# Low parts of the weights: a scalar-engine multiplication and an adding DMA in place of a vector subtraction

## The chip, the cores and the metric

The kernel runs on one core of a Trainium2 chip. A core has TensorE (PE, matrix products), VectorE (DVE), ScalarE (ACT), GpSimd (POOL) and SyncE (SP), each with its own queue of instructions that it takes strictly in order, and 16 DMA engines that are shared by all queues that issue transfers. The metric is the device time of one execution in microseconds (us).

## What is computed

Two layers of a sequence model over 512 tokens of width 1024, all in float32. Each layer has a token mixer (indexer-selected attention beside chunked gated linear attention), a residual with layer norm, a convolutional feed-forward network, and a second residual with layer norm. Cut to what matters here:

```python
def reference(x, positions, w_in, ...):
    for l in range(DEPTH):
        y = hybrid_mixer(x, positions, w_in[l], ..., p_attn[l], p_gla[l], w_mix_out[l], b_mix_out[l])
        x = layer_norm(DN_ALPHA * x + y, ln1_g[l], ln1_b[l])
        y = conv_ffn(x, w_up[l], conv_w[l], conv_b[l], w_down[l])
        x = layer_norm(DN_ALPHA * x + y, ln2_g[l], ln2_b[l])
    return x
```

Nearly all of the arithmetic is products of activations with weight matrices: w_in (1024 x 7256), p_attn, p_gla, w_mix_out, w_up (1024 x 5632) and w_down (2816 x 1024), for each layer.

## The kernel before

Every weight is streamed once, in 286 tiles of 128x1024 float32 (512 KB; two of them are 128x832). TensorE works on a rounded format (float32r), so a float32 operand is split in two: a high part, which is the value rounded, and a low part, which is the value minus the high part. A product is then three matmuls (mm3, lines 148 to 152): high by low, low by high, high by high.

A tile w has both parts side by side: w[:, 0] is the high one and w[:, 1] the low one. A tile's life is: SP issues the load of raw (line 130); ACT casts raw to the high part (line 144, in split); DVE subtracts the high part from raw into the low part (line 145); PE uses w in 24 matmuls of 512 columns (or 48 of 256). There are three buffers for raw (pool wraw) and five for w (pool wsp). So a load waits until raw has been read for the last time, three tiles before, and a cast waits until PE has done with the w of five tiles before.

pump (lines 125 to 135) issues load, cast and subtraction; weight calls it so that up to four tiles are ready ahead of their use, in the order that plan_all has laid down. The split of a tile is emitted at high priority: the framework's scheduler, which sets the order of each engine's queue when the kernel is built, puts it ahead of other work that is ready at the same time. The first tile of all is split in run (in two halves), not in pump. No caller of pump gives its argument parts.

Which of the two parts PE wants first depends on the stage. Where the weight is the moving operand (tm_chunk and closing: mixer projections, output products) the first matmul needs the low part. Where it is the stationary operand (fm_tile) the first needs the high part and the second the low one.

Most stages use a tile in one run and release it. Three places keep four tiles at once: the second half of closing (each of four token blocks goes over the same four tiles), the start of ffn (four tiles of w_up, first over tokens 0 to 255, then over 256 to 511) and the first product of layer 2 (iq, in two halves of the tokens). A closing is followed by one of the other two, so there the five slots come free late.

Beside the weights, POOL has little to do: constants at the start, the power in rstd (line 298; each layer norm of a token block has one, its argument comes from DVE and its result goes back to DVE), and 16 copies of 128 KB in twice (line 484), by DMA from POOL's queue.

Of the kernel before, what the change touches and what calls it, by code (L numbers as in the profile page):

```python
# [10 lines left out]
F32 = mybir.dt.float32  # L11
F32R = mybir.dt.float32r
I32 = mybir.dt.int32
AF = mybir.ActivationFunctionType
ALU = mybir.AluOpType
# [40 lines left out]
class Trunk:  # L56
# [68 lines left out]
    def pump(self, ahead, parts=None):  # L125
        while self.nsp < len(self.seq) and len(self.ready) < ahead:
            key, src, n = self.seq[self.nsp]
            self.nsp += 1
            raw = self.wraw.tile([128, n], F32, name=self.name("raw"), tag="raw")
            self.nc.sync.dma_start(raw.rearrange(src[1], **src[2]) if src[1] else raw, src[0])  # L130
            w = self.wsp.tile([128, 2, n], F32R, name=self.name("w"), tag="w")
            with self.tc.high_priority():
                for c in parts or (slice(0, n),):
                    self.split(w[:, 0, c], w[:, 1, c], raw[:, c])
            self.ready.append((key, w))

    def weight(self, key, keep=0):
# [872 lines left out]
```

## Time and profile before

| what | us |
|---|---|
| median of 3 runs (1798.42 to 1799.81) | 1798.6 |
| the profiled execution, its own time | 1798.15 |
| its span, first to last instruction | 1796.4 |
| PE busy | 1770.9 |
| DVE busy | 1150.0 |
| ACT busy | 758.4 |
| POOL busy | 35.6 |

The span is what the rows of the trace divide; the profiled execution took 1.75 us more than its span. TensorE's granted clock was 0.999 of full speed over the span. "Busy" of PE counts a matmul until its modelled end, so short waits between matmuls are not seen as idle time. In rows of groups and of time lines the operation is written with the program's names, output first: `w<-raw` writes w from raw. A line is that of kernel.py; split's lines 144 (ACT) and 145 (DVE) serve all splits, so weights are told apart by the names w and raw.

### The profile page before, as it was taken

How to read it: one execution, taken by the hardware profiler on the slowest of the kernel's cores; microseconds unless marked ns; L12 is line 12 of the kernel's file. 1: busy time of each engine (PE TensorE's matmuls, PEld its weight loads, DVE VectorE, ACT ScalarE, POOL GpSimd, SP SyncE). 2: the span in 40 equal slices, each digit the busy share in tenths (PEclk: the TensorE clock that was granted, in tenths of full speed). 3: DMA queues.
4: the chain of work that ended last, by engine and by line, in shares of the span. 5: the costliest groups of instructions: out<-in, count | busy, mean ns of one | idle time of the engine just before them, and what ended most of it. 6: DMA issues, size and time to landing. Idle time of an engine off the chain costs nothing.

```text
span 1796.4 us, 21646 instructions
## 1 busy us (share of the span) xinstructions
PE 1770.9 (99%) x8280; PEld 1436.5 (80%) x8280; DVE 1150.0 (64%) x2172; ACT 758.4 (42%) x1154; POOL 35.6 (2%) x57
## 2 busy tenths in 40 slices
PE   9999999999999999999999999999999999999997
PEld 7787787888888888888878877787888888888886
DVE  7899768733476553355768997786335765532556
ACT  6644657522225442144255456574232254422440
POOL 0000000000000000000000001000000000000000
PEclk9999999999999999999999999999999999999999
DMA  6222231233523322232332223212325233223331
GB/s 204 68 81 63 78 97 48 82 95 94 170 76 106 94 94 94 94 95 95 127 120 71 73 69 91 74 59 72 106 93 175 66 111 94 94 94 94 95 115 49
DMA packets 56980, 169.38 MB, mean 94 GB/s; under 512 B 6214, under 2 KB 6470, under 8 KB 56876
## 3 DMA queue, kind: packets, MB, share of 16 engines
q1 hardware_dynamic: 51312, 153.96, 27.5%
q10 hardware_dynamic: 4284, 11.94, 2.0%
q0 software_dynamic: 1280, 2.10, 0.6%
q8 instruction: 65, 1.06, 0.2%
q14 instruction: 39, 0.32, 0.1%
HBM read 161.68 MB, written 4.19 MB: 92 GB/s over the span
## 4 chain that ended last, share of the span: by engine, by line
PE 60%; DVE 5%; issue 3%; ACT 1%; POOL 1%; POOLq 0%; DVEq 0%; ACTq 0%
PE ps L152 19%; PE ps L150 19%; PE ps L151 19%; DVE w L145 1%; DVE u L741 1%; POOL rs L298 1%; PE ps L491 1%; PE ps L492 1%; PE ps L640 0%; DVE u L740 0%; DVE sc L525 0%; DVE bs L734 0%; DVE xT L145 0%; DVE u L853 0%; DVE u L145 0%
## 5 line engine op out<-in xcount | busy, mean ns | idle before, releaser
L145 DVE TENSOR_TENSOR w<-raw,w 128x1024 fp32r<-128x1024 f32 (+2 forms) x287 | 349.6, 1218 | 488.9 <-ACT w L144 488.2
L144 ACT CAST w<-raw 128x1024 fp32r<-128x1024 f32 (+2 forms) x287 | 299.8, 1045 | 482.9 <-PE ps L152 415.8
L150 PE MATMUL ps<-xT,w 128*128 128x512 f32 (+2 forms) x1232 | 475.4, 386 | 0.0
L152 PE MATMUL ps<-xT,w 128*128 128x512 f32 (+2 forms) x1232 | 472.6, 384 | 0.0
L151 PE MATMUL ps<-xT,w 128*128 128x512 f32 (+2 forms) x1232 | 472.2, 383 | 0.0
L152 PEld LDWEIGHTS ps<-xT,w 128*128 128x128 f32 (+1 forms) x1232 | 231.7, 188 | 48.1
L150 PEld LDWEIGHTS ps<-xT,w 128*128 128x128 f32 (+1 forms) x1232 | 231.9, 188 | 45.9
L151 PEld LDWEIGHTS ps<-xT,w 128*128 128x128 f32 (+1 forms) x1232 | 231.9, 188 | 45.4
L150 PE MATMUL ps<-w,u 128*128 128x512 f32 x480 | 190.3, 397 | 0.0
L152 PE MATMUL ps<-w,u 128*128 128x512 f32 x480 | 189.4, 395 | 0.0
L151 PE MATMUL ps<-w,u 128*128 128x512 f32 x480 | 189.3, 394 | 0.0
L150 PE MATMUL ps<-w,xT 128*128 128x512 f32 x448 | 179.7, 402 | 0.0
L152 PE MATMUL ps<-w,xT 128*128 128x512 f32 x448 | 177.9, 397 | 0.0
L151 PE MATMUL ps<-w,xT 128*128 128x512 f32 x448 | 176.6, 394 | 0.0
L144 ACT CAST u<-h 128x512 fp32r<-128x512 f32 x104 | 64.2, 620 | 199.6 <-DVE h L893 111.4
L150 PEld LDWEIGHTS ps<-w,u 128*128 128x128 f32 x480 | 90.4, 188 | 21.1 <-issue 0.3
L152 PEld LDWEIGHTS ps<-w,u 128*128 128x128 f32 x480 | 90.4, 188 | 21.0
L151 PEld LDWEIGHTS ps<-w,u 128*128 128x128 f32 x480 | 90.5, 188 | 20.5
L152 PEld LDWEIGHTS ps<-w,xT 128*128 128x128 f32 x448 | 84.3, 188 | 19.3
L150 PEld LDWEIGHTS ps<-w,xT 128*128 128x128 f32 x448 | 85.0, 190 | 18.0 <-DVE w L145 0.3
L151 PEld LDWEIGHTS ps<-w,xT 128*128 128x128 f32 x448 | 84.5, 189 | 16.2
L145 DVE TENSOR_TENSOR u<-h,u 128x512 fp32r<-128x512 f32 x104 | 71.3, 689 | 38.7 <-ACT u L144 38.4
(200 smaller groups left out, 2076.6 us busy)
## 6 DMA issues: line engine op xcount, KB each, us to landing
raw<-in_w_fm SPq DMA_DIRECT2D x160, 512.0 KB, 3.6
raw<-in_w_tm SPq DMA_DIRECT2D x55, 512.0 KB, 3.6
raw<-in_w_down SPq DMA_DIRECT2D x44, 512.0 KB, 3.4
raw<-in_w_mix_out SPq DMA_DIRECT2D x16, 512.0 KB, 3.4
raw<-in_p_attn SPq DMA_DIRECT2D x8, 512.0 KB, 3.8
u<-in_xT SPq DMA_DIRECT2D x8, 256.0 KB, 5.4
u<-u POOLq DMA_DIRECT2D x16, 128.0 KB, 2.8
u<-in_x ACTq DMA_DIRECT2D x4, 512.0 KB, 6.6
```

The source lines that it names most:

```text
L144: first = self.nc.scalar.copy(hi, src)
L145: self.nc.vector.tensor_sub(lo, src, hi.bitcast(F32))
L150: mm(out, lh, rl, start=start, stop=False)
L151: mm(out, ll, rh, start=False, stop=False)
L152: mm(out, lh, rh, start=False, stop=stop)
L298: self.nc.gpsimd.tensor_tensor(r, ve, self.nhalf[:, :n], ALU.pow)
L491: mm(out, q, k, start=True, stop=False)
L492: mm(out, q, kl, start=False, stop=True)
L741: nc.vector.scalar_tensor_tensor(x[:, c], x[:, c], r, b[:, c], op0=ALU.mult, op1=ALU.add)
```

## The change

In pump, the split of a tile is replaced. ACT casts raw to the high part as before; ACT then writes minus the high part into the low part's place; then a DMA issued from POOL's queue adds raw to what stands there, in place. raw minus high is again what the low part holds. split itself and all other uses of it stay as they are, and so does the first tile.

```diff
             with self.tc.high_priority():
-                for c in parts or (slice(0, n),):
-                    self.split(w[:, 0, c], w[:, 1, c], raw[:, c])
+                if parts:
+                    for c in parts:
+                        self.split(w[:, 0, c], w[:, 1, c], raw[:, c])
+                else:
+                    self.nc.scalar.copy(w[:, 0], raw)
+                    self.nc.scalar.mul(w[:, 1], w[:, 0].bitcast(F32), -1.0)
+                    self.nc.gpsimd.dma_start(w[:, 1], raw.bitcast(F32R), accum_op=ALU.add)
             self.ready.append((key, w))
```

In the changed kernel the cast is line 137, the multiplication 138 and the adding DMA 139; every later line of the old kernel has a number higher by 5. The scheduler lays the queues anew. POOL's queue grows by 285 DMAs, ACT's by 285 activations, DVE's loses 285 subtractions. Names of buffers are numbered in the order in which they are made, so the numbers of the two kernels differ.

ACT's queue at the start of the kernel, where the second, third and fourth weight tiles (raw_121, raw_132, raw_143) and the quarters of x transposed (u) arrive. Before:

```order
L144 CAST w_123<-raw_121 128x1024 [waits DMAHW5_49]
L144 CAST xT<-u_101 128x512 [waits DMAHW6_49]
L144 CAST xT<-u_102 128x512 [waits DMAHW7_49]
L144 CAST w_134<-raw_132 128x1024 [waits DMAHW0_49]
L144 CAST xT<-u_102 128x512 [waits DMAHW1_49]
L144 CAST xT<-u_103 128x512 [waits DMAHW2_49]
L144 CAST w_145<-raw_143 128x1024 [waits DMAHW3_49]
```

The same place in the changed kernel:

```order
L137 CAST w_123<-raw_121 128x1024 [waits DMAHW5_49]
L149 CAST xT<-u_101 128x512 [waits DMAHW6_49]
L138 ACTIVATE w_123<-w_123 128x1024 [waits Activation_49]
L149 CAST xT<-u_102 128x512 [waits DMAHW7_49]
L137 CAST w_135<-raw_133 128x1024 [waits DMAHW0_49]
L149 CAST xT<-u_102 128x512 [waits DMAHW1_49]
L138 ACTIVATE w_135<-w_135 128x1024 [waits Activation_49]
L149 CAST xT<-u_103 128x512 [waits DMAHW2_49]
```

A multiplication stands behind each cast of a weight, with one cast of xT between. PE's queue is the same in both kernels over this stretch.

POOL's queue at the conv-FFN's start in layer 1 (w_4479 is the first tile of w_up, w_4491, w_4503 and w_4701 the next three; rs are the norms of the four token blocks). Before there are only the norms' powers:

```order
L298 TENSOR_TENSOR rs_4441<-rs_4440,nhalf 128x1
L298 TENSOR_TENSOR rs_4492<-rs_4491,nhalf 128x1
L298 TENSOR_TENSOR rs_4550<-rs_4549,nhalf 128x1
L298 TENSOR_TENSOR rs_4608<-rs_4607,nhalf 128x1
L275 MEMSET h_7132 96x512
```

In the changed kernel:

```order
L139 DMA w_4479<-raw_4477 128x1024 [waits DMASW7_49,DMAHW3_49,PE_49,Activation_49]
L303 TENSOR_TENSOR rs_4520<-rs_4519,nhalf 128x1 [waits DVE_49]
L303 TENSOR_TENSOR rs_4571<-rs_4570,nhalf 128x1 [waits DVE_49]
L303 TENSOR_TENSOR rs_4629<-rs_4628,nhalf 128x1 [waits DVE_49]
L139 DMA w_4491<-raw_4489 128x1024 [waits DMASW0_49,DMAHW5_49,PE_49,Activation_49]
L139 DMA w_4503<-raw_4501 128x1024 [waits DMASW1_49,DMAHW6_49,PE_49,Activation_49]
L139 DMA w_4701<-raw_4699 128x1024 [waits DMASW2_49,DMAHW7_49,PE_49,Activation_49]
L303 TENSOR_TENSOR rs_4687<-rs_4686,nhalf 128x1 [waits DVE_49]
```

The last block's power has three adding DMAs ahead of it, which wait for ACT; these stand behind the powers of the first three blocks, which wait for DVE.

DVE's queue at the same place, the norm of the third token block (u_4253 before, u_4324 after). Before:

```order
L297 TENSOR_SCALAR rs_4549<-mv_4547 128x1 [waits DVE_49]
L740 SCALAR_TENSOR_TENSOR u_4253<-u_4253,mv_4547,u_4257 128x512
L145 TENSOR_TENSOR w_4414<-raw_4412,w_4414 128x1024 [waits DMAHW4_49,Activation_49]
L299 TENSOR_TENSOR rs_4551<-rs_4550 128x1 [waits Pool_49]
L740 SCALAR_TENSOR_TENSOR u_4253<-u_4253,mv_4547,u_4257 128x512
L145 TENSOR_TENSOR w_4425<-raw_4423,w_4425 128x1024 [waits DMAHW6_49,Activation_49]
L300 TENSOR_TENSOR rs_4551<-rs_4551,rs_4549 128x1 [waits DVE_49]
L145 TENSOR_TENSOR xT<-ps_4569,xT 128x4x128
L145 TENSOR_TENSOR w_4622<-raw_4620,w_4622 128x1024 [waits DMAHW7_49,Activation_49]
L301 TENSOR_SCALAR rs_4551<-rs_4551 128x1 [waits DVE_49]
```

In the changed kernel:

```order
L302 TENSOR_SCALAR rs_4628<-mv_4626 128x1 [waits DVE_49]
L745 SCALAR_TENSOR_TENSOR u_4324<-u_4324,mv_4626,u_4328 128x512
L304 TENSOR_TENSOR rs_4630<-rs_4629 128x1 [waits Pool_49]
L745 SCALAR_TENSOR_TENSOR u_4324<-u_4324,mv_4626,u_4328 128x512
L305 TENSOR_TENSOR rs_4630<-rs_4630,rs_4628 128x1 [waits DVE_49]
L150 TENSOR_TENSOR xT<-ps_4648,xT 128x4x128 [waits Activation_49]
L306 TENSOR_SCALAR rs_4630<-rs_4630 128x1 [waits DVE_49]
```

Three subtractions of weights that stood between the steps of this norm are gone.

## Rows read from the trace of the kernel before

**Rows 1.** The page: busy time, share of the span and instructions by engine.

```profile
PE 1770.9 (99%) x8280; PEld 1436.5 (80%) x8280; DVE 1150.0 (64%) x2172; ACT 758.4 (42%) x1154; POOL 35.6 (2%) x57
```

**Rows 2.** Windows: us, PE, PEld, DVE, ACT, POOL busy (x instructions), PEclk, DMA share, GB/s.

```profile
0.00:20.00 20.00, 18.47 (x70) 14.64 (x71) 13.87 (x32) 12.27 (x17) 3.44 (x18) 1.00 0.84 290
100.00:240.00 140.00, 135.73 (x697) 109.16 (x696) 119.52 (x295) 72.28 (x115) 7.60 (x10) 1.00 0.28 83
500.00:548.00 48.00, 46.97 (x312) 42.52 (x311) 36.43 (x70) 15.77 (x21) 3.91 (x4) 1.00 0.26 77
548.00:840.00 292.00, 292.00 (x1260) 236.73 (x1259) 151.62 (x179) 106.68 (x133) 1.51 (x3) 1.00 0.30 96
...
1740.00:1796.40 56.40, 46.73 (x202) 37.49 (x200) 32.84 (x65) 6.12 (x7) 3.93 (x4) 0.95 0.21 75
```

**Rows 3.** Groups by line and form: busy us, mean ns | idle before, releasers.

```profile
L145 DVE TENSOR_TENSOR w<-raw,w 128x1024 fp32r<-128x1024 f32 x283 | 346.2, 1223 | 486.4 <-ACT w L144 485.7
...
L144 ACT CAST w<-raw 128x1024 fp32r<-128x1024 f32 x283 | 296.8, 1049 | 480.5 <-PE ps L152 415.8 <-issue 41.1 <-DMA u<-in_ln_b 9.1
...
L198 ACT ACTIVATE u<-u 128x1024 f32<-128x1024 f32 x6 | 6.1, 1056 | 0.1
```

**Rows 4.** Waits: engine, line, waited for: us in total, times, longest us.

```profile
ACT w L144 <- PE ps L152: 415.8, 213, 5.0
...
SPq L130 <- DVE w L145: 1354.5, 243, 17.8
...
PEld ps L461 <- ACT w L144: 2.3, 4, 0.9
```

**Rows 5.** Time line of DVE and PE: start us, us, engine, line, operation [idle before].

```profile
162.01 1.22 DVE L145 TENSOR_TENSOR w<-raw,w 128x1024 fp32r<-128x1024 f32 x1
...
163.98 0.35 PE L150 MATMUL ps<-u,u 128*128 128x256 f32 x1 [0.73 <-DVE sh L592]
...
173.05 0.39 PE L150 MATMUL ps<-u,u 128*128 128x256 f32 x1 [1.43 <-DVE u L145]
...
52.53 0.73 PE L404 MATMUL ps<-u,tri 128*128 128x512 f32 x2 [0.92 <-DVE u L145]
```

**Rows 6.** The page's DMA queues, and issues with median us to landing.

```profile
q1 hardware_dynamic: 51312, 153.96, 27.5%
...
q0 software_dynamic: 1280, 2.10, 0.6%
...
raw<-in_w_fm SPq DMA_DIRECT2D x160, 512.0 KB, 3.6
...
u<-u POOLq DMA_DIRECT2D x16, 128.0 KB, 2.8
```

**Rows 7.** Time line of the start: second and third weight tiles on ACT, DVE, PE.

```profile
8.76 1.05 ACT L144 CAST w<-raw 128x1024 fp32r<-128x1024 f32 x1 [0.83 <-DMA raw<-in_w_tm]
9.72 1.13 ACT L144 CAST xT<-u 128x512 fp32r<-128x512 f32 x2
...
9.84 1.23 DVE L145 TENSOR_TENSOR w<-raw,w 128x1024 fp32r<-128x1024 f32 x1 [0.92 <-ACT w L144]
...
11.12 0.19 PEld L150 LDWEIGHTS ps<-w,xT 128*128 128x128 f32 x1 [0.31 <-DVE w L145]
...
12.51 1.22 DVE L145 TENSOR_TENSOR w<-raw,w 128x1024 fp32r<-128x1024 f32 x1 [0.24 <-ACT w L144]
```

**Rows 8.** Time line at the start of conv-FFN (layer 1) and of layer 2.

```profile
517.84 1.05 ACT L144 CAST w<-raw 128x1024 fp32r<-128x1024 f32 x1 [0.86 <-PE ps L152]
...
525.08 0.28 PE L150 MATMUL ps<-xT,w 128*128 128x256 f32 x1
...
529.52 0.14 DVE L297 TENSOR_SCALAR rs<-mv 128x1 f32<-128x1 f32 x1
...
891.36 1.05 ACT L144 CAST w<-raw 128x1024 fp32r<-128x1024 f32 x1 [0.82 <-PE ps L152]
...
898.57 0.39 PE L150 MATMUL ps<-w,xT 128*128 128x512 f32 x1
```

## The prediction

> **What bounds the kernel now.** I read the page first. TensorE is busy for 1770.9 of 1796.4 us, DVE for 1150.0, ACT for 758.4 [rows 1]. So the change can only matter where PE waits for something, now or afterwards. The windows of chosen stretches come next [rows 2]. In the stretch from 548 to 840 us (layer 2 has a twin of it) PE is busy for the whole window: 1260 matmuls in 292 us are 0.232 us each, and a weight tile, used for 24 of them, lasts 5.56 us. In the mixer's stretch (100 to 240, with a twin in layer 2) PE is idle for 4.3 us while DVE is busy for 119.5 of 140 us. The last 56.4 us hold 9.7 us of PE's idle time, behind the closing norms, and the first 20 us 1.5. Of the 25.5 us that PE is idle at all, 14.3 are left in between: no relief of DVE can show a gain beyond these, apart from waits shorter than a matmul's drain, which the rows hide.
>
> The lines view gives the edited step [rows 3]: 283 full subtractions on DVE of 1.22 us each, behind as many ACT casts of 1.05 us. The waits [rows 4] show who holds whom. ACT's cast waits for PE's last use of a weight slot (415.8 us, 213 times); the loads on SP's queue wait for the subtraction, which frees the raw buffer (1354.5 us). Both are stocks: with five slots, a cast that starts when PE leaves a slot has four weights, 22.2 us, before PE wants it, and cast and subtraction need 2.3.
>
> **The change, part by part.** Every tile but the first goes through the new branch (no caller names parts): 285 of them.
>
> Removed: 285 DVE subtractions, 346.2 us for the 283 full ones. In the steady stretches this is worth nothing, since PE does not wait there. It is worth something where a subtraction stands on DVE ahead of work that PE awaits. Such places are in [rows 5]: a subtraction begins at 162.01, the split that PE awaits comes behind it, and PE idles 0.73 us; the same pattern costs 1.43 us before 173.05 and 0.92 before 52.53. The first two I count once for each layer. At the start of each conv-FFN four subtractions stand inside the norm chain (the order above shows three of them), and PE's idle time there, 500 to 548 us, is 1.03 us [rows 2]. Together 2 x (0.73 + 1.43) + 0.92 + 2 x 1.03 = 7.3 us. The ends are 0 (the next late thing, an ACT copy, takes over) and 14.3.
>
> Added on ACT: 285 multiplications of a 128x1024 tile, each like the activation of that shape, 1.06 us [rows 3]; ACT goes from 758 to some 1060 us, 59% of the span. It is hidden under PE except where PE waits for ACT behind a weight's cast: the transposes of L461 do so four times, 2.3 us in all [rows 4]. One multiplication more ahead of each is 4 x 1.06 = 4.2 us. Ends: 0, and twice that because ACT is fuller. I take 4.2.
>
> Added on the DMA engines: 285 transfers that read raw and the tile and write the tile. No row shows an adding transfer, so I bound it. A load holds the 16 engines for 0.30 of 5.56 us, or 1.67 us [rows 2]. An add reads two operands of that size: I take 2 x 1.67 = 3.3 us, because its bytes are those of two loads. The lower end is 1.67, one load. The upper end uses the rate of GpSimd's own queue, 0.6% of the engines for 2.10 MB against 27.5% for 153.96 MB [rows 6]: 1.6 times as long for each byte, so 5.3 us. The time to landing also has a fixed part: a GpSimd copy of 128 KB lands after 2.8 us [rows 6], of which 0.7 are its data at that queue's rate. So an add lands 2.1 + 3.3 = 5.4 us after its issue, with ends 2.8 and 7.4. The Trainium skill's page "Collectives: The Full Stack", section "The bandwidth ceiling", says that a reducing transfer runs at half the rate of a copy because of its two source reads and not because of the addition; no row here shows that, and by it the engine time is the same 3.3. The Trainium skill's page "DMA: Bandwidth & Descriptors", section "Anatomy of one DMA", gives a GpSimd transfer 2.0 us plus its bytes at 436 GB/s, an estimate of 3.2 us for 512 KB; the 2.8 us for 128 KB agree within half a microsecond, and by that figure the stall at the start below would be 3.4 us and the whole sum near 1803.
>
> In a steady stretch the load and the add hold the engines for 1.67 + 3.3 = 5.0 of each 5.56 us. This fits, at 0.9 of the engines. From the cast to the landed add is 1.05 + 1.06 + 5.4 = 7.5 us of the 22.2 that are there. The raw buffer is now free only after the add, so with the next load's 3.6 us [rows 6] a raw buffer's round is 11.1 us; with three buffers 16.7 are there. So the steady stretches cost nothing, at the price of that stock.
>
> Where the stock is not there, the added time shows.
>
> The start [rows 7]: the second weight's cast ends at 9.81, its subtraction at 11.07, and PE uses the low part at 11.12, after 0.31 us of waiting: there is no stock at all. In the new order one half of xT is cast (0.57) before the multiplication, which ends at 11.35; the add lands at 16.75, 5.6 us late, with ends of 3.0 and 7.6. The engines are 0.84 busy in the first 20 us [rows 2], so I take 6, with ends of 3 and 9. PE's rows there are unchanged and in order, so nothing fills the hole. The next tile was ready at 13.73 and wanted one weight's time after 11.12, at 16.7, so its stock of 3 us and the hole's 6 cover its own add.
>
> The three places where four or five tiles are kept at once: both starts of the conv-FFN and the start of layer 2. There the slot comes free late. At 517.84 the cast begins (1.05), a cast of xT follows (0.57 as at the start) and ends at about 519.4, the multiplication at 520.4, the add lands at 525.8; PE's first matmul with that tile is at 525.08 [rows 8], and its second, 0.12 us later, needs the low part: 0.6 us late. For layer 2: 891.36, 893.95, 899.35 against 898.57, 0.8 late. The next two adds follow at 3.3 us each, while PE wants a tile after 24 matmuls, 2.9 us at this half width, so the delay grows by 0.4 a tile. ACT then stands at the cast of the tile after these, whose load has had to wait for the first add; the two casts of xT for the last token block are queued behind it, and PE's second pass needs them. I take 1.5 us a place, 4.5 in all. With adds of 5.3 us the third one would be 5 us late: ends 0 and 15.
>
> GpSimd's queue: rstd's power (L298) waits for DVE with adds queued behind it, and stands itself behind adds. The new order puts the last norm's power behind three adds, the last of which can be issued at about 524.7 (after 520.4 ACT has two casts and two multiplications ahead of it, 4.2 us), while DVE delivered its input at 529.5 before [rows 8] and will do so some 4.9 us earlier without four subtractions: a draw, at nothing.
>
> Sum against the profiled execution's own time of 1798.15 us (span 1796.4 and 1.75 around it; the median of the runs is 1798.6): 6 + 4.5 + 4.2 - 7.3 = 7.4, so 1805.5 us. All lower ends together would give 1787, all upper ends 1831.
>
> **Rivals.** First, DVE's relief decides, and the kernel is faster. For it: DVE is 85% busy in the mixer's stretch, and the rows show subtractions ahead of PE's waits. Against it: 14.3 us is all there is, and the start takes 3 back even at its lower end. With the start at its lower end of 3 and the other losses at nothing it decides from a gain of 6.6 us (3.6 below the runs' uncertainty and 3 for the start); a gain of 11 gives 1790. Second, the DMA engines become the bound. Above 3.9 us of engine time for an add, load and add need more than 5.56 us and PE waits for weights throughout. For it: GpSimd's queue is the slower one for each byte. Against it: its copies touch only 64 partitions, and nothing shows an addition to cost more than its reads. At the upper end, 7.0 against 5.56 us, the two stretches of 292 us alone (105 weights) lose 147 us: 1945 or more. Third, the losses and the gain cancel: 6 at the start against 7.3 from DVE, with the other two terms near nothing, gives 1797 to 1800, no difference.
>
> **How the numbers follow.** A difference under 0.2%, 3.6 us, is about what a measurement of this kernel cannot tell from none. The forecast, a few us lost, has 0.45 above that bound (1802 to 1831). The cancelling case has 0.27, the faster one 0.12, the DMA-bound one 0.16. So faster 0.12, same 0.27, slower 0.61. The range leaves out the DMA-bound case and the end of the faster one: 1793 to 1831.
>
> **What would show it.** Right: a hole of some 6 us in PE at about 11 to 17 us; full PE windows in the middle of the conv-FFN with a DMA share near 0.9; ACT near 1060 us and DVE near 800; the idle times of [rows 5] gone. Wrong: PE waiting for adds in the steady stretches (the DMA-bound case), a hole at the start under 3 us, or PE's waits for ACT grown by far more than 4 us.

## The result, and the profile after

The changed kernel takes 1849.3 us (median of 4 runs, 1847.2 to 1856.6) against 1798.6: a ratio of 1.0286, with a 95% interval of 1.0274 to 1.0298. It is slower by 51 us where 7 were forecast, and outside the range. The profiled execution took 1847.2 us, its span is 1845.5.

The page after: busy times (compare [rows 1]), the DMA queues (packets, MB, share of 16 engines) and the median landings of one DMA (compare [rows 6]), and the two new lines of the change (compare [rows 3]).

```profile
PE 1789.1 (97%) x8280; PEld 1442.2 (78%) x8280; DVE 829.0 (45%) x1887; ACT 1031.4 (56%) x1439; POOL 279.0 (15%) x342
...
q0 software_dynamic: 42320, 151.34, 43.3%
q1 hardware_dynamic: 51312, 153.96, 26.7%
...
L139 POOL DMA_DIRECT2D w<-raw x285 | 244.3, 857 | 1463.4 <-ACT w L138 1192.2
L138 ACT ACTIVATE w<-w 128x1024 fp32r<-128x1024 f32 x285 | 300.0, 1054 | 3.2
...
w<-raw POOLq DMA_DIRECT2D x283, 512.0 KB, 5.4
raw<-in_w_fm SPq DMA_DIRECT2D x160, 512.0 KB, 4.4
```

The parts came out much as priced. DVE is down by 321 us, ACT up by 273, an adding DMA lands 5.4 us after its issue, and it holds the 16 engines for (43.3 - 0.6)% of 1845.5 us over 285, or 2.8 us. TensorE pays in two ways: it is idle for 56.4 us of the span instead of 25.5, and the same 8280 matmuls are busy for 18.2 us longer. The two are the whole 49 us of the span.

Windows of the changed kernel (us, then busy us of PE, PEld, DVE, ACT, POOL with instructions, granted clock, DMA share, GB/s; compare [rows 2]):

```profile
8.00:12.00 4.00, 3.09 (x14) 2.18 (x12) 1.67 (x5) 3.37 (x6) 0.23 (x1) 1.00 1.04 411
12.00:16.00 4.00, 0.00 (x0) 0.00 (x0) 2.07 (x3) 4.00 (x6) 2.17 (x3) 0.91 1.02 279
16.00:20.00 4.00, 2.77 (x7) 2.22 (x8) 0.87 (x3) 1.32 (x2) 0.85 (x1) 0.50 1.02 229
20.00:24.00 4.00, 4.00 (x15) 3.17 (x14) 2.73 (x15) 1.78 (x2) 1.13 (x2) 0.73 1.03 251
20.00:60.00 40.00, 38.12 (x162) 29.95 (x161) 14.44 (x61) 27.62 (x37) 6.56 (x8) 0.93 0.90 213
570.00:862.00 292.00, 292.00 (x1255) 235.77 (x1254) 91.83 (x127) 158.46 (x185) 45.14 (x54) 1.00 0.85 192
900.00:976.00 76.00, 65.84 (x285) 51.56 (x285) 34.68 (x97) 34.02 (x46) 12.04 (x14) 0.91 0.64 165
```

Three things are to be seen. The steady conv-FFN (570 to 862) is as full as before, with 1255 matmuls in 292 us against 1260, at a DMA share of 0.85. The start has its hole (12 to 16), and then a second price: after the hole the granted clock is 0.50, 1.2 instead of 2.4 GHz, and the next four us still have a mean of 0.73. And the DMA engines stay at 0.90 from 20 to 60 us. Around the change of layers (900 to 976) PE loses 10 us to idling, and the clock is 0.91.

What PE, ACT and the load queue wait for (us in total, times, longest; compare [rows 4]):

```profile
SPq L130 <- DMA w<-raw: 1680.1, 282, 21.7
...
ACT w L137 <- DMA raw<-in_w_fm: 33.5, 13, 7.8
ACT w L137 <- DMA raw<-in_w_mix_out: 20.1, 2, 10.5
ACT w L137 <- DMA raw<-in_w_tm: 13.9, 5, 5.4
ACT w L137 <- DMA raw<-in_w_small: 11.8, 2, 8.4
...
PE ps L155 <- DMA w<-raw: 17.0, 5, 6.1
PE ps L156 <- DMA w<-raw: 4.5, 1, 4.5
PE ps L383 <- DVE u L386: 4.1, 1, 4.1
PE ps L155 <- ACT h L707: 3.7, 2, 1.8
PE ps L409 <- DVE u L150: 3.0, 3, 1.2
```

Nearly every load waits for an add to land (282 waits), since that is what frees its raw buffer. ACT's casts wait 79.3 us for loads; before these waits were 7.1 us. PE's matmuls wait for an adding DMA six times only, 21.5 us in all.

To see where the loss lies, take the first matmul of each weight tile before and after and split the delay by stretch. All tables below are made so, from one profiled execution each, in us against the kernel before; where the runs of a kernel spread over 7 to 16 us, a cell can differ from run to run. "Closing a" is the end of layer 1's output product with the first conv-FFN tiles, "b" the end of its down product, "c" is "a" for layer 2.

```
                     start mixer1 clos.a  FFN1 clos.b layer2 mixer2 clos.c  FFN2
changed kernel       +12.4   +2.5   +4.5  +0.8   +4.6  +14.7   +3.6   +5.2  +1.3
```

Before the experiments, the theory was this. PE pays where it has no stock of split weights: the added latency shows there, and each hole costs a second time by the clock. The rivals were that ACT's second pass makes everything behind it late, and that the adding DMAs slow all transfers everywhere.

### The profile page after: what moved, and what is told of

The parts are those of the page before. It is cut to its first block, busy times and chain, and to the rows that moved or that the text cites. A ratio compares the mean times of both kernels' runs of the same rounds, so it can differ in the third digit from the quotient of the medians.

```text
span 1845.5 us, 22241 instructions
## 1 busy us (share of the span) xinstructions
PE 1789.1 (97%) x8280; PEld 1442.2 (78%) x8280; DVE 829.0 (45%) x1887; ACT 1031.4 (56%) x1439; POOL 279.0 (15%) x342
## 3 DMA queue, kind: packets, MB, share of 16 engines
q0 software_dynamic: 42320, 151.34, 43.3%
## 4 chain that ended last, share of the span: by engine, by line
PE 72%; ACT 9%; DVE 7%; DMA 7%; issue 4%; POOL 1%; SPq 0%; POOLq 0%; ACTq 0%; DVEq 0%
PE ps L155 23%; PE ps L157 22%; PE ps L156 22%; ACT w L137 2%; DMA w<-raw 2%; ACT w L138 2%; DVE sc L530 2%; DVE m L529 1%; DMA raw<-in_w_fm 1%; DMA raw<-in_w_mix_out 1%; DVE sc L521 1%; PE ps L645 1%; ACT u L602 1%; PE ps L496 1%; DMA raw<-in_w_tm 1%
## 5 line engine op out<-in xcount | busy, mean ns | idle before, releaser
L137 ACT CAST w<-raw 128x1024 fp32r<-128x1024 f32 x285 | 298.2, 1047 | 479.2 <-PE ps L157 399.4
L139 POOL DMA_DIRECT2D w<-raw x285 | 244.3, 857 | 1463.4 <-ACT w L138 1192.2
L138 ACT ACTIVATE w<-w 128x1024 fp32r<-128x1024 f32 x285 | 300.0, 1054 | 3.2
L155 PE MATMUL ps<-w,u 128*128 128x512 f32 x480 | 193.1, 402 | 9.3 <-DMA w<-raw 9.3
L157 PE MATMUL ps<-w,u 128*128 128x512 f32 x480 | 191.2, 398 | 0.0
L156 PE MATMUL ps<-w,u 128*128 128x512 f32 x480 | 191.1, 398 | 0.0
L155 PE MATMUL ps<-w,xT 128*128 128x512 f32 x448 | 181.8, 407 | 8.6 <-DMA w<-raw 7.7
L885 DVE SCALAR_TENSOR_TENSOR h<-ps,cw,h 128x511 f32<-128x511 f32 x88 | 66.0, 750 | 261.0 <-ACT h L884 260.7
L157 PE MATMUL ps<-w,xT 128*128 128x512 f32 x448 | 179.3, 400 | 0.0
L156 PE MATMUL ps<-w,xT 128*128 128x512 f32 x448 | 178.8, 399 | 0.0
L155 PEld LDWEIGHTS ps<-w,u 128*128 128x128 f32 x480 | 91.3, 190 | 32.0 <-DMA w<-raw 10.6
L155 PEld LDWEIGHTS ps<-w,xT 128*128 128x128 f32 x448 | 85.6, 191 | 29.2 <-ACT xT L149 7.2
L157 PEld LDWEIGHTS ps<-w,xT 128*128 128x128 f32 x448 | 85.5, 191 | 19.7
```

What stands on the lines that cost most here:

```text
L137: self.nc.scalar.copy(w[:, 0], raw)
L138: self.nc.scalar.mul(w[:, 1], w[:, 0].bitcast(F32), -1.0)
L139: self.nc.gpsimd.dma_start(w[:, 1], raw.bitcast(F32R), accum_op=ALU.add)
L155: mm(out, lh, rl, start=start, stop=False)
L156: mm(out, ll, rh, start=False, stop=False)
L157: mm(out, lh, rh, start=False, stop=stop)
```

## Which part of the change costs

Four runs take the change apart. The lines of the edited step, with the runs that leave a line out or put one in; e9 also has PE read the high part in the low part's place:

```diff
 self.nc.scalar.copy(w[:, 0], raw)
-self.nc.scalar.mul(w[:, 1], w[:, 0].bitcast(F32), -1.0)              # e9, e2
-self.nc.gpsimd.dma_start(w[:, 1], raw.bitcast(F32R), accum_op=ALU.add)  # e9, e1, e3
+self.nc.vector.tensor_scalar(w[:, 1], w[:, 0].bitcast(F32), -1.0, None, op0=ALU.mult)  # e2
+self.nc.gpsimd.dma_start(w[:, 1], raw.bitcast(F32R))                 # e3
```

> The kernel before with the low parts of the weights left out: no subtraction by DVE, no second ACT pass, no adding DMA, and PE reads the high part twice (so values differ; as many matmuls and weight loads). It is DVE's relief alone, at no cost elsewhere. The prediction's term for it was 7.3 us (0 to 14.3): by that 1785 to 1796 us, with 1792 for the term itself. Rival 'the queue moves on' (what waited for DVE then waits for the next engine in line): 1797 to 1800 us.

> Of the changed kernel only the adding DMA is left out: ACT casts the weight and negates the cast, and the low part is then minus the high part, without the raw weight added (so its values differ). ACT carries its whole new load, DVE none of the subtractions, and the raw buffer is free once the cast has read it. Theory 'DMA' (the adding DMA's landing time and the raw buffer it holds make PE wait at the places without stock): 1790 to 1802 us, the start's hole of 6.3 us gone. Rival 'ACT' (the second ACT pass delays everything else in ACT's order): 1835 us or more, with the PE waits on ACT of the changed kernel still there.

> The GpSimd DMA copies the raw weight over the low part instead of adding it (the addition is left out, so the low part's values differ); ACT's two passes, the waits and the raw buffer's life stay. If the DMA's latency in the chain and the held raw buffer are what counts, the time falls only by the difference in landing (5.4 us with the addition, some 4 without): 1830 to 1845 us. If the engine time of the addition (2.8 us per weight against 1.7 for the load's) and the crowding it makes at the restarts is what counts: 1800 to 1818 us. Rival 'ACT': 1845 to 1850 us.

> The negation is done by DVE instead of ACT; the adding DMA stays as in the changed kernel. ACT has its load of before, DVE about its load of before. Theory 'DMA': 1840 to 1858 us, as the changed kernel. Rival 'ACT': 1800 to 1812 us.

Measured: 1795.6 without low parts (0.9981, 0.9972 to 0.9991), 1808.4 with ACT's second pass (1.005, 1.0035 to 1.0065), 1818.8 with a copying DMA (1.0106, 1.0089 to 1.0123), 1850.2 with DVE negating (1.0281, 1.0266 to 1.0297).

```
                     start mixer1 clos.a  FFN1 clos.b layer2 mixer2 clos.c  FFN2
e9 no low parts       +0.2   -1.6   -1.4  +1.0   +0.9   -0.6   -2.1   -1.5  +1.3
e1 ACT's pass, no DMA +1.3   +4.1   -1.4  +1.3   +0.9    0.0   +4.6   -1.5  +1.3
e3 copying DMA        +8.3   +3.5   -1.4  +1.3   +0.9   +5.9   +2.1   -1.4  +1.3
e2 DVE negates       +18.3   -0.2   +9.8  +0.5   +1.1  +14.6   -0.6   +7.8  +0.8
```

Read as a ladder, each against the kernel before as measured beside it: DVE's relief gives 3.2 us; ACT's second pass takes 12.1 (to +8.9); a DMA that copies takes 10.3 more (+19.2); the addition itself takes 31.5 (+50.7). The 12.1 us fell outside both expectations for e1, which had ACT's pass either free or dear; e3's 1818.8 lies 0.8 us above the range for the addition's engine time as what counts. ACT's pass costs in the two mixers, and the time line of e1 shows how (start us, us, engine, line, operation [idle before]):

```profile
215.50 0.30 PE L465 MATMUL ps<-ident,h 128*128 128x128 f32 x1 [0.98 <-ACT u L601]
215.56 0.48 PE L154 MATMUL ps<-w,xT 128*128 128x512 f32 x1
216.96 0.30 PE L465 MATMUL ps<-ident,h 128*128 128x128 f32 x1 [0.92 <-ACT w L137]
217.01 0.48 PE L155 MATMUL ps<-w,xT 128*128 128x512 f32 x1
...
217.85 0.63 PE L155 MATMUL ps<-w,xT 128*128 128x512 f32 x1
218.28 0.63 PE L156 MATMUL ps<-w,xT 128*128 128x512 f32 x1
```

Two waits of a microsecond on ACT's order, and then matmuls that start 0.43 us apart instead of 0.23: the small holes, too, are paid twice. The waits for the merge's ACT step (PE on ACT h, 3.7 us in two) are new in e1 and stand in the changed kernel as well; before there were none.

The run e2 warns against adding up: with ACT back at its load of before, the time does not fall at all. Its table shows that ACT's price does not vanish beside the adding DMA: the mixers lose nothing any more (-0.2 and -0.6 against +2.5 and +3.6). But the start and closings a and c lose more than in the changed kernel. At a closing DVE now stands at a negation, whose cast waits for its load, with the steps of a norm behind it that PE's transposes need (DVE's line, then PE's):

```profile
554.13 0.69 DVE L138 TENSOR_SCALAR w<-w 128x1024 fp32r<-128x1024 f32 x1 [4.19 <-ACT w L137]
...
556.21 1.09 PE L756 MATMUL ps<-ident,u 128*128 128x128 f32 x4 [4.72 <-DVE u L746]
```

PE waits for such steps 17.5 us in seven times; the changed kernel's list of waits has none. What ACT's queue is spared, DVE's now loses behind loads that land late.

Of the addition, the copying run shows what it doubles. From its page (queue, then landing):

```profile
q0 software_dynamic: 42320, 151.34, 23.2%
...
w<-raw POOLq DMA_DIRECT2D x283, 512.0 KB, 3.2
```

A copy of the same bytes holds the engines for (23.2 - 0.6)% of 1817.7 us over 285, or 1.4 us, against 2.8 for the add, and lands after 3.2 us against 5.4. That agrees with what the Trainium skill's page "Collectives: The Full Stack" (section "The bandwidth ceiling") says of a ring's reducing step: for its two source reads it runs at half the rate of a copying one. The 3.2 us are also what the Trainium skill's page "DMA: Bandwidth & Descriptors" (section "Anatomy of one DMA") gave as an estimate; it holds for the copy, and not for the add.

## Where it costs

Here the old split is used for some tiles and the new path for the others; `pump` asks for the key:

```diff
+        what = key[1]                         # stocked of e7
+        if what == "fm":
+            return not FM["up"] <= key[2] < FM["up"] + 4
+        return not (what in ("iq", "small", "gk") or what in ("wout", "wdB") and key[2] == 1)
...
+                if self.stocked(key):         # cast, multiplication, adding DMA; else the old split
```

> The changed kernel with the old split (ACT cast, DVE subtraction) for the tiles that have no stock behind them: iq, small and gk of each layer, the second half of the two closing products, and the first four tiles of each conv-FFN; 246 of 286 tiles keep the negation and the adding DMA. Theory 'no stock' (the loss lies where the adding DMA's chain is longer than the stock): the holes at the start, at the closings and at the layer change go, and what is left is what ACT's second pass alone costs: 1802 to 1812 us. Rival 'crowding everywhere' (the adding DMAs of all tiles slow the loads): 1825 us or more.

> The changed path only in the conv-FFN's steady stretches (up tiles from the fifth, both halves of the first down product, first half of the second), the old split everywhere else. Theory 'hidden in steady stretches': 1797 to 1803 us, with PE busy for the whole of a middle FFN window and the DMA share there near 0.84. Rival 'crowding everywhere': 1806 us or more.

> The changed kernel with the old split for the iq and small tiles of each layer alone (10 of 286 tiles). Theory 'the layer's first tiles have no stock': the start's 12 us and the layer change's 15 us go, the three closings' 14 us and the waits on ACT stay: 1818 to 1828 us. If the loss at the layer change comes from before it (adds and loads queued at the end of the FFN): 1833 us or more.

Measured: 1805.8 (1.0034, 1.0021 to 1.0048), 1797.5 (0.999, 0.998 to 0.9999) and 1840.1 (1.0217, 1.0195 to 1.0239).

```
                     start mixer1 clos.a  FFN1 clos.b layer2 mixer2 clos.c  FFN2
e7 old at starts      +1.4   +2.4   -0.9  +1.3    0.0   +1.3   +3.4   -1.1  +0.4
e8 new in FFN only    +0.4    0.0   -0.9  +1.3    0.0    0.0    0.0   -1.2  +0.7
e11 old in iq, small +11.2   +4.7   +0.7  +1.3   +2.9   +7.6   +3.6   +8.6  +1.4
```

The first two are as expected. With the old split at the tiles that have no stock, 44 of the 51 us are gone, although 244 tiles still use the adding DMA (e7's list of keys leaves out 42, so 244, and not the 246 of the expectation); what stays is ACT's part in the mixers. In the steady conv-FFN alone the change costs nothing. So the rival of crowding everywhere falls.

The third missed its 1818 to 1828. With the old split for the first five tiles of each layer, PE starts as early as before, but the start still loses 11.2 us: the next tile, gk, now comes late. In the time line of e11, ACT stands at a weight's cast for 5.82 us until its load lands; a small load of gate weights, issued by ACT behind that cast, holds it for 2.89 us more; and PE waits 6.39 us for the ACT copy after these. So the loss at the start is not tied to the first tile. At the change of layers the five tiles do count: the waits for the adds of iq and small are gone, and closing b and layer 2 lose 10.5 us instead of 19.3. At the start, what matters is the rate at which a stock can be built at all. In the changed kernel's time line of ACT, the casts after the start are these:

```profile
14.80 1.04 ACT L137 CAST w<-raw 128x1024 fp32r<-128x1024 f32 x1
20.73 0.89 ACT L137 CAST w<-raw 128x832 fp32r<-128x832 f32 x1 [3.41 <-DMA raw<-in_w_small]
25.24 1.05 ACT L137 CAST w<-raw 128x1024 fp32r<-128x1024 f32 x1 [2.70 <-DMA raw<-in_w_tm]
29.45 1.05 ACT L137 CAST w<-raw 128x1024 fp32r<-128x1024 f32 x1 [0.40 <-DMA raw<-in_w_tm]
36.33 1.05 ACT L137 CAST w<-raw 128x1024 fp32r<-128x1024 f32 x1 [4.74 <-DMA raw<-in_w_tm]
41.06 1.06 ACT L137 CAST w<-raw 128x1024 fp32r<-128x1024 f32 x1
```

Five tiles in 26.3 us are 5.3 us each, while PE uses one in 5.6: there is nothing to build a stock from. Before, the casts of tiles two to seven stood at 8.8 and 20.3, 2.3 us each. The closings show the same from the other side. At 495 to 520 us the rows of x and of the norm's parameters (3.1 MB) come in. The DMA view of 480 to 530 (KB each, median us to landing):

```profile
w<-raw POOLq DMA_DIRECT2D x7, 512.0 KB, 6.5
raw<-in_w_mix_out SPq DMA_DIRECT2D x4, 512.0 KB, 10.6
u<-in_x ACTq DMA_DIRECT2D x4, 512.0 KB, 10.9
```

The 10.6 us are one load of the output product, issued at 503.12, the only one of the four whose landing the trace gives. Before, the output product's loads landed after 3.4 us, ahead of x's rows, and a load beside them after 5.4. This load keeps ACT's cast waiting, and PE then waits for the add of the same tile (ACT's line, then PE's):

```profile
513.83 1.05 ACT L137 CAST w<-raw 128x1024 fp32r<-128x1024 f32 x1 [9.61 <-DMA raw<-in_w_mix_out]
...
520.71 0.80 PE L155 MATMUL ps<-w,u 128*128 128x512 f32 x1 [3.27 <-DMA w<-raw]
```

## Crowded engines, a held buffer, or the landing

Three effects come with the adding DMA: it crowds the engines, it holds the raw buffer until it lands, and PE waits for its landing. Two runs were meant to add one effect each to e1:

```diff
 self.nc.scalar.mul(w[:, 1], w[:, 0].bitcast(F32), -1.0)
+self.nc.gpsimd.dma_start(sink, w[:, 0], accum_op=ALU.add)       # e13: HBM scratch
+self.nc.gpsimd.dma_start(sink, raw[:, :8])                      # e14
+self.nc.gpsimd.dma_start(sink, raw[:, 8:16], accum_op=ALU.add)  # e14
```

> The run without the adding DMA (1808 us, the low part being minus the high part), and beside it a GpSimd DMA per weight that adds the 512 KB of the cast weight onto scratch rows in HBM. PE never waits for it and it does not read the raw buffer: the DMA engines are crowded, nothing else. Theory 'crowding' (the adding DMA's engine time delays the loads at the restarts, and so the casts and what is behind them): 1818 us or more, loads landing in more than 4 us. Rival 'chain' (what costs is the raw buffer held and the landing that PE waits for): 1806 to 1812 us.

> The run without the adding DMA, and beside it two GpSimd DMAs per weight, one after the other, that read 8 columns of the raw buffer each: the raw buffer is held for about two small landings after the negation, the DMA engines move next to nothing more, and PE never waits for it. Theory 'held buffer' (the ring of three is what makes the loads late): 1814 us or more, with ACT waiting on loads at the closings. Rival 'crowding' or 'landing': 1806 to 1812 us.

Measured: 1843.8 for e13 (1.0251, 1.0211 to 1.029, against the kernel before) and 1819.1 for e14 (1.0112, 1.0097 to 1.0127), so 35 and 11 us above e1's 1808.4.

```
                     start mixer1 clos.a  FFN1 clos.b layer2 mixer2 clos.c  FFN2
e13 crowded engines  +15.3   +2.6   +5.1  +0.5   +1.8   +4.4   +4.2  +10.8  +0.5
e14 held buffer      +10.7   +4.2   -0.4  +1.3   +1.6    0.0   +2.6   -0.4  +1.3
```

The page of e13 (queues, then landings):

```profile
q0 software_dynamic: 42320, 151.34, 45.4%
...
raw<-in_w_fm SPq DMA_DIRECT2D x160, 512.0 KB, 5.2
...
raw<-in_w_down SPq DMA_DIRECT2D x44, 512.0 KB, 7.4
```

Neither run adds its effect alone. In e13 the adds hold the engines for 2.9 us per weight, and loads land late. But other work waits for them than in the changed kernel: ACT's casts of weights wait 4.5 us for loads in all, against 79.3. At the start ACT stands for the small load of gate weights, and PE behind it; at the closings PE's transposes wait for the norms (15.2 us, six times), twice because x's rows came late, and twice because the power of a norm stood in POOL's queue behind an add to the scratch. The wait at the start, and one in POOL's queue with what it costs DVE:

```profile
47.84 0.62 ACT L290 CAST r<-h 96x512 fp32r<-96x512 f32 x1 [12.39 <-DMA h<-in_w_gate]
...
1461.89 0.85 POOL L145 DMA_DIRECT2D sink<-w  x1 [4.79 <-DMA sink<-w]
...
1463.36 0.16 DVE L310 TENSOR_TENSOR rs<-rs 128x1 f32<-128x1 f32 x1 [3.92 <-POOL rs L309]
```

So crowded engines can cost as much as the whole change, but e13 does not show by which of the changed kernel's waits. The expectation for e14 has the small DMAs behind the negation, but they read raw as soon as its load has landed, and in a steady stretch both have landed before the cast begins. Only for 23 of the 285 tiles does the second one land after the cast, for the first ten of them 5 to 9 us after it, much as the add does in the changed kernel (7.25, the median of all tiles). So the loads of e14 wait for casts far more often than for these DMAs (us in total, times, longest):

```profile
SPq L131 <- ACT w L138: 1354.2, 248, 18.9
SPq L131 <- DMA sink<-raw: 164.8, 60, 9.8
```

Its 11 us are the price of the held buffer at the start, where it is held (10.7 against 1.3 in e1); for the closings and the change of layers e14 shows next to nothing.

At layer 2's start the changed kernel loses 14.7 us, e13 4.4 and e14 0.0. There PE waits 1.59 us at 928.30 for an add, and 4.45 at 939.36 for the add of the tile small: these are landings in PE's chain, and e11 has neither. It waits 4.11 more at 967.68, for a DVE step of the decay task. That step stands behind others that waited for ACT, and ACT had stood at a cast until its load landed (PE's line, then ACT's):

```profile
939.36 0.72 PE L156 MATMUL ps<-xT,w 128*104 128x512 f32 x1 [4.45 <-DMA w<-raw]
...
960.04 1.05 ACT L137 CAST w<-raw 128x1024 fp32r<-128x1024 f32 x1 [5.38 <-DMA raw<-in_w_tm]
```

How the 42 us between e1 and the changed kernel divide among crowding, the held buffer and the landing stays open. What is shown is that a copy in place of the add, which is shorter in all three, takes 31.5 of them back.

A fourth raw buffer is the obvious remedy for the held one. Room for it was made by shrinking two small pools, and that moved the weight tiles in the memory:

> The changed kernel with four raw buffers instead of three (room made by two instead of three small buffers of the attention's values and four instead of six of the tiny ones). If the raw buffer, held from the load until the add has landed, is what takes the lead away, every load is issued one tile (5.6 us) earlier: the holes at the end of the three closings (3.4, 2.0 and 4.4 us with their clock) go and those at the change of layers shrink: 1820 to 1838 us. If only the add's own landing counts: 1844 to 1852 us. Rival 'ACT': 1845 to 1852 us.

Measured: 1814.4 (1.0083, 1.0065 to 1.01), 35 us back. But its table has -8 us in each steady conv-FFN, where the changed kernel lost nothing. It also lies below every expected range. So some 16 of the 35 us are not the ring's, and a control was needed.

## The spacing of the matmuls

The control keeps three raw buffers and puts the tiles where they were in e4:

```diff
+        pad = pool("pad", 1).tile([128, 352], F32, name="pad", tag="pad")   # e5, e6, e10
         self.wraw = pool("wraw", 3)
+        pad = pool("pad", 1).tile([128, 96], F32, name="pad", tag="pad")    # e12
         self.wsp = pool("wsp", 5)
```

> The kernel before with 1408 bytes per partition left empty ahead of the raw buffers, and nothing else: the raw and the split weight tiles then start at the same offset, modulo 2048, as in the kernel with four raw buffers (1664 instead of 256). There a weight tile took PE 5.44 us in every steady stretch (matmul to matmul 227 ns), against 5.575 us (228 to 241 ns) in the kernel before. Theory 'address' (the tiles' place in the memory sets the spacing): 5.44 us per tile here too and 1774 to 1784 us. Rival 'ring' (the fourth raw buffer, or the smaller pools, gave it): 5.575 us and 1797 to 1801 us.

> The changed kernel with the same 1408 empty bytes and three raw buffers: the control of the run with four. Theory 'raw lead': against the run with four raw buffers (1814 us) it stays 10 us or more longer, with the holes of the layer change back at 14 us or more: 1824 to 1832 us. If the fourth buffer gave nothing and all of its 35 us were the spacing of the matmuls: 1810 to 1818 us. If the addresses do nothing: 1846 to 1852 us.

> The kernel before with 384 empty bytes per partition between the raw buffers and the split weight tiles: the weight tiles alone move, to 640 modulo 2048, which is 128 modulo 512 as xT's place is; the raw buffers stay. If it is the weight tiles' offset modulo 512 against xT's that sets the matmuls' spacing: 5.44 us per tile and 1772 to 1778 us. If the raw buffers' place or the offset modulo 2048 counts: 1797 to 1801 us.

> The changed path only in the conv-FFN's steady stretches, with the 1408 empty bytes ahead of the raw buffers. The empty bytes alone gave 1773.9 us, the changed path in the FFN alone was within 2 us of the kernel before: 1770 to 1776 us if the two are independent.

Measured: the kernel before with empty bytes 1773.9 (0.9856, 0.9841 to 0.9871), with 384 of them ahead of the weight tiles alone 1773.2 (0.9857, 0.984 to 0.9873); the changed kernel with them 1823.3 (1.014, 1.0123 to 1.0157); the changed path in the FFN only, with them, 1768.4 (0.9829, 0.9815 to 0.9844).

The steady conv-FFN of the kernel before with empty bytes (e5), to be held against the 1260 matmuls of [rows 2], and its time line (start us, us, engine, line, operation):

```profile
544.00:836.00 292.00, 292.00 (x1292) 241.68 (x1291) 156.98 (x185) 109.56 (x136) 1.50 (x3) 1.00 0.31 98
...
600.04 0.39 PE L153 MATMUL ps<-xT,w 128*128 128x512 f32 x1
600.27 0.39 PE L151 MATMUL ps<-xT,w 128*128 128x512 f32 x1
600.49 0.39 PE L152 MATMUL ps<-xT,w 128*128 128x512 f32 x1
```

A matmul every 0.226 us instead of 0.232, at the same granted clock of 1.00: 25 us on the whole kernel, with nothing moved but the raw buffers and the weight tiles, and in e12 the weight tiles alone. With this known, e4 reads differently. At equal addresses modulo 2048 the fourth raw buffer is worth 1823.3 - 1814.4, or 9 us (10 or more were expected), with runs from 1810.6 to 1817.6 against 1817.0 to 1827.9; the two profiled executions took 1817.6 and 1817.0, so where the 9 us lie can't be shown.

The run e10 is 30 us faster than the kernel before, and 1.6 below its expected range. Most of it is the empty bytes; against e12 on the same chip (1773.2, runs from 1772.9 to 1774.2) the changed path in the conv-FFN gives 4.7 us more (1768.2 to 1768.7). Of these, 1.4 and 1.2 lie at the two conv-FFN starts, where fewer subtractions stand among DVE's work on the norms; another 1.4 lie in the second mixer, which has the old path in both, so their cause is not shown.

## The prediction, point by point

- **Prices of the parts: right.** Engine time of an add 2.8 us (3.3 forecast, 1.67 to 5.3), its landing 5.4 (5.4), ACT 1031 us (1060), DVE 829 (800).
- **Steady stretches: right.** PE is busy for the whole of the middle conv-FFN at a DMA share of 0.85 (0.9), and e8 shows the path free there. The rival with the DMA engines as the bound throughout did not come.
- **The start: the hole right, its price not.** PE waited 6.14 us before 17.23 where 6 were forecast, and it waited for no other add there: the next tile's stock and the hole did cover its own add, as the prediction says. But the start lost 12.4 us. After the hole, and after a second one of 1.88 us at 45.73, PE was busy for 8.3 us at a granted clock of 0.50, which cost about 4. The second hole was for an ACT copy that stood behind casts, which stood for their loads. The step that failed is the term itself: it let the loss end with the first hole, at full clock, and looked at one tile, not at the rate of the ones that follow and at what stands behind their casts on ACT.
- **The places without stock: the term that missed most.** Counted were three, at 1.5 us each, 4.5 in all (0 to 15). Measured were 14.7 at layer 2's start and 4.5, 4.6 and 5.2 at the three closings, 29 us. This is the step of the prediction that missed by most: a place was priced as one late add at an unchanged load, and the closings ahead of it at nothing. The first tiles of the conv-FFN did what was forecast or less. The hole came one tile earlier, at the last tile of the closing product, which the prediction had taken as steady. Its raw buffer's round of 11.1 us against 16.7 was worked out with a load of 3.6 us; there one load took 10.6, beside x's rows and the adds on the same engines. At layer 2's start ACT's cast waited 5.38 us for a load too.
- **ACT: too small.** Forecast 4.2 (0 to 8.4), measured 12.1 without the DMA. The four waits counted were the right kind; missing were the merge's step and the slow matmuls after each wait.
- **DVE's gain: right where it was counted.** Of the idle times of [rows 5], the two ahead of L150's matmuls are gone in the changed kernel, the one ahead of L404 (now L409) is not: 3.0 us in three waits. Forecast 7.3; e9 has 1.6 and 2.1 in the mixers and 1.4 and 1.5 at the conv-FFN starts, 6.6 in all. The kernel as a whole gained 3.2, in the main because the steady stretches ran 1 us longer each: their matmuls stood 0.233 instead of 0.232 us apart.
- **GpSimd's queue: a draw, as forecast, as far as the trace shows.** No run puts the power step and the adds on different queues, but DVE waited for the power 9.8 us in 15 times, against 11.4 in 16 before, never longer than 1.8. In e13, where an add to the scratch can wait for an earlier one, it was no draw (21.2 us).
- **The range.** 1831 was all upper ends together. It failed because the places were priced one by one, with PE at full clock and loads at their median landing. The direction, and the parts' prices, held.

## What to carry to other kernels

A buffered stream has two numbers, the depth that hides a latency and the rate at which the depth is refilled after it was used up. A longer chain is free in the steady state and dear after each place where the stock is gone; price it there by the round of the smallest ring and by transfers at the landing that they have in that stretch, not at their median. Price an idle hole of TensorE with the slow clock behind it: here 18 of 49 us were matmuls that took longer. Some 14.5 of them lie in eight stretches with a granted clock of 0.50, in which PE was busy for 29 us; each of these comes with a wait of PE of 1.8 to 6.1 us, though one wait of 1.84 us (at 350.6) has no such stretch. About 2 are the wider spacing in the steady stretches. And when a control moves buffers, look at a stretch that should not change.

## What the runs showed of the hardware

- The place of the weight tiles in a partition sets the spacing of 128x512 matmuls: 0.232 us with the tiles at 256 modulo 2048 bytes, 0.2265 with them at 1664 and at 640 (xT stays at 128; the addresses are added up from the sizes of the program's pools, no trace has them). The five runs with other places than 256 (e4, e5, e6, e10, e12) show 5.44 us per weight tile in the steady conv-FFN, all runs at 256 show 5.57 to 5.60. It needs no other place of the raw buffers (e12). Both places that were better are 128 modulo 512, as xT's is; whether that is the rule wasn't tried.
- An adding DMA costs the engines twice what a copy does (2.8 against 1.4 us for 512 KB), and lands after 5.4 us against 3.2.
- In five of the six kernels in which adds run beside the loads everywhere or nearly so (the changed kernel, e4, e6, e11, e13), runs of one kernel spread over 7 to 16 us (1836.2 to 1852.1 in e13); the four runs of e2, which has the same adds, lay within 2.1, and the first runs of the kernel before within 1.4. Why e2 does not spread is not shown.
